# Output operands prepared as the merged tiles come, the merge's first pages loaded ahead of later weights, and four PSUM banks for the spatial mixing

## The chip, the cores and the metric

One core of one Trainium2 chip. The metric is the device time of one execution of the program in microseconds, the median of three runs.

## What is computed

One layer of a decoder block on a sequence of 1024 tokens of width 1024, all in float32. `h = rms_norm(x)` goes through one wide projection, which gives the inputs of three branches and three merge gates:

```python
u, v  -> y_a = (u * (causal spatial mixing of layer_norm(v) + bias)) * silu(a_z)   # 768 wide
q,k,v -> y_b = (dilated window attention, 3 patterns, combined) * silu(b_z)        # 256 wide
m_q   -> y_m = (attention into 256 memory tokens) * silu(m_z)                      # 512 wide
gates  = sigmoid(g.reshape(bn, s, 3, 1024) + gate_b)
merged = gates[0] * (y_a @ proj_a) + gates[1] * (y_b @ proj_b) + gates[2] * (y_m @ proj_m)
x      = x + merged @ w_out
```

## The kernel before

Every product of matrices in this part is made of three matmuls (`mm3`, L159 to L161): each operand is split into a high half (ACT, L137) and a low half (DVE, L138), and high x high, high x low and low x high are added in one PSUM bank. So each loaded weight piece (`piece`, load at L142 through SP's queue) and each page of `y` costs one operation of ACT and one of DVE before TensorE (PE) can use it. `pj` is the PSUM tag with four banks for the products; `sc` and `tr` are tags with two banks each. SP's DMA queue and each engine's queue run in order; that order is fixed when the program is built, mostly but not strictly by the order in the source.

From about 867 us to the end the kernel does the following.

The wide projection writes gate tiles and `y` pages to DRAM; its last pair of column tiles ends at 870 us. Then the merge runs in three passes over eight column tiles `dt` of the result, two halves `i` each, so 16 products a pass. `gates_m` (memory branch, 12 matmuls a product) loads the branch's first pages with `load_y(0, ...)` (L1109, tiles `ym00l` and `ym01l`, split by `split_y`), takes eight weight pieces pm0 to pm7 that were queued as `steps` (L1010) and multiplies by the gate tile `merged[dt]` in place (L1159). `gates(1, ...)` (window branch, 6 matmuls a product) and `gates(0, ...)` (gating branch, 18 matmuls) take a gate tile `tg` and weights from `prepare`, one tile ahead; DVE multiplies the product by the gate into `tg` (L1204), which also empties the PSUM bank; then the result is added to `merged[dt]`: by POOL in the second pass (L1208), and in the third pass by an accumulating DMA from POOL's queue (L1206) for tiles 0 to 6 and by DVE for tile 7 (L1208).

During the first two passes `spatial` makes the six `ya` tiles: matmuls into a `mx` bank (L1242), DVE scales and adds the bias (L1243, empties the bank), POOL multiplies by `us` (L1247), and `split` makes the halves `yah`/`yal` by ACT and DVE. `pump` releases these steps between the products of the passes.

The third pass runs over the tiles in the order 0, 4, 1, 5, 2, 6, 3, 7. After each one `merged_done` calls `right_sums`. The output projection is a seven-product scheme for blocks of 2 x 2: its right operands (1, 5, 3, 2, 6, 7, 4) are blocks of `merged` and sums of them, where tiles `k` and `k + 4` form a pair. `right_sums(k + 4)` makes for pair `k` the halves `ro1`, a subtraction (L1301), `ro5`, `ro3`, `ro2` and three more sums (L1305 to L1307); `half_split` makes the high half on ACT (L1288) and the low half on DVE (L1289). The operands 6, 7 and 4 follow with `right_late`, at once for pairs 0 and 1 and between the output's products for 2 and 3. `places` lists the buffer of each operand in the order of the calls: freed pages of the `y` tiles, freed merged tiles, and slices of `rpool`, whose two buffers held `ya0` and `ya1`. The left operands come from `w_out` by `next_steps`.

The output is a list of products (`jobs`), 12 matmuls of 256 columns each. The first four (rows 0 and 1, operands 1 and 5) run in two goes, `k` = 0 to 2 for all four and `k` = 3 after that (`partial`); they are written to the four `pj` banks that the last products of the third pass had. The results are added to the residual tiles `xr`, which take the three buffers of the `tg` ring, and stored.

## Time and profile before

| | |
|---|---|
| time, median of 3 runs | 1119.93 us (1119.44 to 1121.22) |
| the profiled execution | 1120.26 us, of it 1118.5 us span |
| mean granted clock of PE | 0.994 |
| busy share of the span | PE 98%, DVE 71%, ACT 46%, POOL 17% |
| DMA moved | 157.57 MB, 141 GB/s over the span |

The times of the rows below are from this one execution, counted from the start of its span. PE is the matmul engine, PEld its weight load, DVE the vector, ACT the scalar and POOL the GpSimd engine; SP's queue issues most of the loads. A row of the waits names the engine that stood still, its instruction, and behind the arrow the instruction whose end it waited for. A busy time is that of the instructions' own durations, and neighbours on one engine overlap a little.

### The profile page before, as it was taken

The page shows a single profiled execution, that of the slowest core. Times are in us where ns is not written, and L with a number is a line of the kernel's source. Part 1 is how long each engine was busy: PE and PEld are TensorE (multiplying, and loading weights), DVE is VectorE, ACT ScalarE, POOL GpSimd, SP SyncE. Part 2 cuts the span into 40 slices and gives each one's busy share as a digit, 9 for nine tenths or more (in the row PEclk, how much of TensorE's full clock was granted, in tenths as well). Part 3 has the DMA queues.
Part 4 walks back from the last instruction along what each step waited for, and adds up shares of the span by engine and source line. Part 5 has one row for each costly group of instructions (what it writes and reads, how often), then busy time and mean ns, then how long its engine had stood idle before and what let it go on. Part 6 is the DMA issues. An engine that isn't in the chain of part 4 may idle for free.

```text
span 1118.5 us, 18302 instructions
## 1 busy us (share of the span) xinstructions
PE 1092.7 (98%) x6680; PEld 955.9 (85%) x6680; DVE 794.1 (71%) x1701; ACT 514.0 (46%) x1123; POOL 195.7 (17%) x250
## 2 busy tenths in 40 slices
PE   8989999999999999999999999999999999998998
PEld 7879999999988887888888888888888787886998
DVE  6999899856687766656555656687885467568863
ACT  6553333223245543755665554666564562134320
POOL 0000431321000002011111111111111026511232
PEclk9999999999999999999999999999999999999999
DMA  7222322454242423444434325455544975665432
GB/s 236 76 96 91 128 86 96 144 190 151 72 142 94 129 98 119 143 147 153 128 121 136 124 95 181 123 180 157 166 132 132 335 273 160 173 161 136 142 107 83
DMA packets 84558, 157.57 MB, mean 141 GB/s; under 512 B 9605, under 2 KB 30708, under 8 KB 84468
## 3 DMA queue, kind: packets, MB, share of 16 engines
q1 hardware_dynamic: 68164, 106.87, 30.6%
q0 software_dynamic: 14864, 47.05, 13.0%
q10 hardware_dynamic: 1440, 2.49, 0.6%
q8 instruction: 52, 0.85, 0.3%
q14 instruction: 38, 0.31, 0.1%
HBM read 106.84 MB, written 48.22 MB: 139 GB/s over the span
## 4 chain that ended last, share of the span: by engine, by line
PE 86%; DVE 5%; DMA 4%; issue 3%; POOL 1%; ACT 1%; SPq 0%; POOLq 0%; DVEq 0%; ACTq 0%
PE t L159 12%; PE t L161 12%; PE t L160 11%; PE n L160 7%; PE n L159 7%; PE n L161 7%; PE po L606 3%; PE pp L159 2%; DMA merged<-tg 2%; PE pp L161 2%; PE pp L160 2%; PE po L160 2%; PE po L159 2%; PE po L161 2%; PE pt L599 1%
## 5 line engine op out<-in xcount | busy, mean ns | idle before, releaser
L159 PE MATMUL t<-th,wh_t 128*128 128x512 f32 x336 | 135.2, 402 | 0.0
L161 PE MATMUL t<-th,wl_t 128*128 128x512 f32 x336 | 132.0, 393 | 0.0
L160 PE MATMUL t<-tl,wh_t 128*128 128x512 f32 x336 | 131.4, 391 | 0.0
L159 PE MATMUL n<-wh_n,th 128*128 128x256 f32 x384 | 108.2, 282 | 0.0
L161 PE MATMUL n<-wh_n,tl 128*128 128x256 f32 x384 | 107.6, 280 | 0.0
L160 PE MATMUL n<-wl_n,th 128*128 128x256 f32 x384 | 107.6, 280 | 0.0
L161 PEld LDWEIGHTS t<-th,wl_t 128*128 128x128 f32 x336 | 63.1, 188 | 14.5
L159 PEld LDWEIGHTS n<-wh_n,th 128*128 128x128 f32 x384 | 73.3, 191 | 1.5 <-issue 0.9
L160 PEld LDWEIGHTS t<-tl,wh_t 128*128 128x128 f32 x336 | 63.3, 188 | 12.8
L159 PEld LDWEIGHTS t<-th,wh_t 128*128 128x128 f32 x336 | 63.3, 188 | 12.3
L160 PEld LDWEIGHTS n<-wl_n,th 128*128 128x128 f32 x384 | 72.1, 188 | 0.2 <-issue 0.2
L161 PEld LDWEIGHTS n<-wh_n,tl 128*128 128x128 f32 x384 | 72.2, 188 | 0.0
L159 PE MATMUL t<-H2h,wh_t 128*128 128x512 f32 x168 | 67.8, 404 | 0.0
L137 ACT CAST wh_t<-ws_t 128x512 fp32r<-128x512 f32 x86 | 51.8, 619 | 33.3 <-PE n L161 11.8
L161 PE MATMUL t<-H2h,wl_t 128*128 128x512 f32 x168 | 65.9, 392 | 0.0
L160 PE MATMUL t<-H2l,wh_t 128*128 128x512 f32 x168 | 65.5, 390 | 0.0
L138 DVE TENSOR_TENSOR wl_t<-ws_t,wh_t 128x512 fp32r<-128x512 f32 x86 | 58.2, 685 | 10.0 <-ACT wh_t L137 9.9
L1069 DVE TENSOR_TENSOR o<-t,sa 128x512 f32<-128x512 f32 x63 | 43.3, 687 | 29.5 <-PE t L161 25.1
L1038 POOL DMA_DIRECT2D scr_g<-o x48 | 26.1, 544 | 191.9 <-ACT o L1024 167.1
L939 POOL TENSOR_TENSOR on<-on,nss 128x1024 f32<-128x1024 f32 x12 | 26.2, 2205 | 173.4 <-DVE nss L134 116.0
L159 PE MATMUL n<-wh_n,H2h 128*128 128x256 f32 x192 | 54.9, 286 | 0.1
L160 PE MATMUL n<-wl_n,H2h 128*128 128x256 f32 x192 | 54.3, 283 | 0.0
(382 smaller groups left out, 3185.1 us busy)
## 6 DMA issues: line engine op xcount, KB each, us to landing
ws_t<-in_w_t SPq DMA_DIRECT2D x64, 256.0 KB, 3.5
scr_g<-o POOLq DMA_DIRECT2D x48, 256.0 KB, 2.7
tg<-scr_g SPq DMA_DIRECT2D x16, 512.0 KB, 3.9
ws_n<-in_w_n SPq DMA_DIRECT2D x24, 256.0 KB, 3.3
wr_n<-in_w_n SPq DMA_DIRECT2D x24, 256.0 KB, 3.3
scr_qk<-on POOLq DMA_DIRECT2D x12, 512.0 KB, 4.3
bx<-scr_qk SPq DMA_DIRECT2D x24, 256.0 KB, 3.3
wr_t<-in_w_t SPq DMA_DIRECT2D x20, 256.0 KB, 3.5
```

The lines of the kernel that those rows point to most:

```text
L137: A.copy(out=hi, in_=y)
L138: (eng or V).tensor_tensor(out=lo, in0=y, in1=hi.bitcast(F32), op=ALU.subtract)
L159: T.matmul(o, lhsT=ah, rhs=bh, start=first, stop=False)
L160: T.matmul(o, lhsT=ah, rhs=bl, start=False, stop=False)
L161: T.matmul(o, lhsT=al, rhs=bh, start=False, stop=last)
L599: T.transpose(p2[:, h * P:(h + 1) * P], c.pr[h // 2][:, h % 2, b * P:(b + 1) * P], ident)
L606: T.matmul(po[:, 64 * h:64 * h + 64], lhsT=c.pT[b][:, h * P:(h + 1) * P], rhs=mb.v[:, (t - nk + 1 + b) % 3, 64 * h:64 * h + 64], start=b = ...
L939: G.tensor_tensor(out=v, in0=v, in1=ss[:, 16 * ORD[q]:16 * ORD[q] + 16].unsqueeze(2) .to_broadcast([P, 16, 64]), op=ALU.mult)
L1038: G.dma_start(out=t[:, h], in_=d)
L1069: V.tensor_tensor(out=o[q], in0=psum, in1=s, op=ALU.add)
```

## The change

The program has the same matmuls in the merge and in the output. (A) Only pm0 to pm3 are queued as steps; pm4 to pm7 and the first `prepare` of each later pass are issued after the DMA of `ym01l` (`issue_after`). (B) The `mx` products alternate between the tags `sc` and `tr`. (C) `right_sums` makes operands 1 and 5 of pair `k` when tile `k` is merged and the rest when tile `k + 4` is, each handed out one tile behind except after tiles 3 and 7; tile 3 is added by DVE as tile 7 was; operands 1 and 5 of pair 3 lie in the `tg` ring; the first four output products run `k` = 0 to 3 in one go; the residual tiles take two slices of one `rpool` buffer; and the sum `s` of the left operands is split from the two that follow it, so that piece 5 of the output comes before them.

```diff
--- before.py
+++ after.py
@@ -336,9 +336,11 @@
             for b in blocks:
                 w[b] = load((11, 21, 22, 12).index(b))
 
-        def sums():
+        def first():
             w["s"] = extra()
             V.tensor_tensor(out=w["s"], in0=w[21], in1=w[22], op=ALU.add)
+
+        def rest():
             V.tensor_tensor(out=w[21], in0=w[11], in1=w[21], op=ALU.subtract)
             V.tensor_tensor(out=w[11], in0=w["s"], in1=w[11], op=ALU.subtract)
 
@@ -346,7 +348,7 @@
             V.tensor_tensor(out=w[12], in0=w[12], in1=w[11], op=ALU.subtract)
 
         return {"load": lambda: loads(11, 12, 21, 22), "11": lambda: loads(11), "12": lambda: loads(12),
-                "2": lambda: loads(21, 22), "sums": sums, "last": last,
+                "2": lambda: loads(21, 22), "s": first, "rest": rest, "last": last,
                 1: lambda: ready(w[11], 1), 2: lambda: ready(w[12], 2), 3: lambda: ready(w[12], 3), 4: lambda: ready(w[22], 4), 5: lambda: ready(w["s"], 5),
                 6: lambda: ready(w[11], 6), 7: lambda: ready(w[21], 7)}
 
@@ -402,7 +404,7 @@
         n = len(ps_)
         ahead.append(ps_)
         nxt = len(ahead)
-        steps.extend((n, step(*keys)) for keys in ((1,), (2,), ("sums", 6), (7, ("11",)), (5,), (4, ("12",)),
+        steps.extend((n, step(*keys)) for keys in ((1,), (2,), ("s", "rest", 6), (7, ("11",)), (5,), (4, ("12",)),
                                                    ("last", 3, ("2",))))
 
     tstack = ExitStack()
@@ -1007,7 +1009,7 @@
         V.scalar_tensor_tensor(out=avs[:, KT:], in0=mv[:, :, 0], scalar=-1.0, in1=avs[:, :KT],
                                op0=ALU.mult, op1=ALU.mult)
 
-    for dt in range(KT):
+    for dt in range(4):
         steps.append((1, lambda dt=dt: prepared.append(piece(w_pm[dt], 512, f"p2{dt}"))))
 
     with tc.tile_pool(name="ppool", reuse_waits="tile", bufs=1, side="right") as pp_:
@@ -1106,7 +1108,7 @@
 
         places.append([[page([P, 2, 512], f"{name}{i}{hp}{d}", F32R) for hp in range(n)] for d in "hl"])
         for hp in range(n):
-            nc.sync.dma_start(out=places[i][1][hp].bitcast(F32), in_=scr[:, 2 * hp:2 * hp + 2, 512 * i:512 * i + 512])
+            last[0] = nc.sync.dma_start(out=places[i][1][hp].bitcast(F32), in_=scr[:, 2 * hp:2 * hp + 2, 512 * i:512 * i + 512])
 
     def split_y(i, places, k):
         hi, lo = (places[i][d][k // 2][:, k % 2, :] for d in range(2))
@@ -1130,6 +1132,7 @@
         nc.sync.dma_start(out=merged[dt][:, t], in_=scr_g[2][dt][:, t])
 
     load_y(0, ym, scr_ym, 2, "ym")
+    first_pages = last[0].ins
     for i in range(4):
         split_y(0, ym, i)
     for dt in range(KT):
@@ -1143,12 +1146,16 @@
 
     def gates_m():
 
-        w = []
+        w, late_w = [], deque()
         for i in range(2):
             t = slice(512 * i, 512 * i + 512)
             for dt in range(KT):
-                if i == 0:
+                if i == 0 and dt < 4:
                     w += take(1, 4)
+                    with tc.issue_after(first_pages):
+                        late_w.append(piece(w_pm[dt + 4], 512, f"p2{dt + 4}"))
+                elif i == 0:
+                    w.append(late_w.popleft())
                 pp = ps.tile([P, 512], F32, name=f"pp2{dt}{i}", tag="pj", bufs=4)
                 for k in range(4):
                     c = slice(k * P, (k + 1) * P)
@@ -1188,7 +1195,8 @@
                 wk_ += [(ph[:, c * P:(c + 1) * P], pl[:, c * P:(c + 1) * P]) for c in range(n)]
             ahead.append((tg, wk_))
 
-        prepare(order[0])
+        with tc.issue_after(first_pages):
+            prepare(order[0])
         for n, dt in enumerate(order):
             if n + 1 < KT:
                 prepare(order[n + 1])
@@ -1202,7 +1210,7 @@
                     pump()
                 m = merged[dt][:, t]
                 V.scalar_tensor_tensor(out=tg[:, t], in0=tg[:, t], scalar=1.0, in1=pp, op0=ALU.add, op1=ALU.mult)
-                if br == 0 and dt < 7:
+                if br == 0 and dt not in (3, 7):
                     G.dma_start(out=m, in_=tg[:, t], accum_op=ALU.add)
                 else:
                     (G if br else V).tensor_tensor(out=m, in0=m, in1=tg[:, t], op=ALU.add)
@@ -1233,7 +1241,7 @@
                                      for d in "hl"))
                 yas.append(lambda half, y=yav[i]: tuple(a[:, 512 * half:512 * half + 512] for a in y))
             yh, yl = yav[i]
-            pm = ps.tile([P, 512], F32, name=f"mx{i}{h}", tag="sc")
+            pm = ps.tile([P, 512], F32, name=f"mx{i}{h}", tag=("sc", "tr")[h])
             mt = p1([P, 512], f"mt{i}{h}", "mt", 2)
             for c4 in range(4):
                 j = 4 * h + c4
@@ -1265,6 +1273,7 @@
     tq = ctx.enter_context(tc.tile_pool(name="tq", reuse_waits="tile", bufs=1))
     pg = lambda pool: lambda n: pool.tile([P, 2, 512], F32R, name=n, tag="pg")
     mg = lambda n: p1([P, 2, 512], n, "mg", 8, tm, F32R)
+    tg_place = lambda n: p1([P, 2, 512], n, "tg", 3, tm, F32R)
     rp = []
 
     def half_r(n):
@@ -1275,8 +1284,8 @@
         return rp[-1][:, 1]
 
     places = ([pg(ypool)] * 8 + [pg(t2)] * 2 + [lambda n: p1([P, 2, 512], n, "pg", 3, tq, F32R)] * 3 + [pg(t2)]
-              + [mg] * 4 + [half_r] * 4 + [pg(ypool)] * 5 + [pg(t2)])
-    spare = [pg(t2)] * 2 + [mg] * 2 + [lambda n: p1([P, 2, 512], n, "tg", 3, tm, F32R)]
+              + [mg] * 4 + [tg_place] * 2 + [half_r] * 2 + [pg(ypool)] * 5 + [pg(t2)])
+    spare = [pg(t2)] * 2 + [mg] * 2 + [tg_place]
     right_o = {}
     late = deque()
     PORDER = (1, 5, 3, 2, 6, 7, 4)
@@ -1292,14 +1301,15 @@
 
     def right_sums(dt):
 
+
+        k = dt % 4
+        b11, b12 = merged[k][:, 0:512], merged[k][:, 512:S]
         if dt < 4:
+            right_o[1, k] = half_split(b11, f"ro1{k}")
+            V.tensor_tensor(out=b11, in0=b12, in1=b11, op=ALU.subtract)
+            right_o[5, k] = half_split(b11, f"ro5{k}")
             return
-        k = dt - 4
-        b11, b12 = merged[k][:, 0:512], merged[k][:, 512:S]
         b21, b22 = merged[dt][:, 0:512], merged[dt][:, 512:S]
-        right_o[1, k] = half_split(b11, f"ro1{k}")
-        V.tensor_tensor(out=b11, in0=b12, in1=b11, op=ALU.subtract)
-        right_o[5, k] = half_split(b11, f"ro5{k}")
         right_o[3, k] = half_split(b22, f"ro3{k}")
         right_o[2, k] = half_split(b21, f"ro2{k}")
         V.tensor_tensor(out=b12, in0=b22, in1=b12, op=ALU.subtract)
@@ -1337,7 +1347,7 @@
     def next_steps(c, n):
 
         for p in osteps[c]:
-            for key in ((1,), ("sums", 5), (2, "last", 3), (), (6,), (7,), (4,))[n]:
+            for key in ((1,), ("s", 5), ("rest", 2, "last", 3), (), (6,), (7,), (4,))[n]:
                 p[key]()
 
     def begin(c):
@@ -1346,8 +1356,13 @@
             p["load"]()
         next_steps(c, 0)
 
+    waiting = []
+
     def merged_done(dt):
-        right_sums(dt)
+
+        waiting.append(dt)
+        while waiting and (dt in (3, 7) or len(waiting) > 1):
+            right_sums(waiting.pop(0))
         if dt == 3:
             begin(0)
             next_steps(0, 1)
@@ -1357,34 +1372,19 @@
     late = deque(sorted(late, key=lambda t: PORDER.index(t[0])))
     jobs = [(0, j, n) for js in ((0, 1), (2, 3)) for ns in (range(2), range(2, 7)) for j in js for n in ns]
     jobs += [(1, j, n) for j in range(4) for n in range(7)]
+    xrs = rpool.tile([P, 2, 2, 512], F32, name="xrs", tag="r")
     tiles = {}
     done = 3
-
-    def partial(c, j, n, ks):
-        q = PORDER[n]
-        if (c, j, n) not in accs:
-            accs[c, j, n] = ps.tile([P, 512], F32, name=f"po{c}{j}{q}",
-                                    **(dict(tag="sc") if q in (2, 3) else dict(tag="pj", bufs=4)))[:, :256]
-        acc = accs[c, j, n]
-        for k in ks:
-            r, (lh, ll) = right_o[q, k], left_o[q, k // 2]
-            w = slice(256 * (k % 2), 256 * (k % 2) + 256)
-            t = slice(j * P, (j + 1) * P)
-            mm3(acc, r[:, 0, t], r[:, 1, t], lh[:, w], ll[:, w], k == 0, k == 3)
-        return acc
-
-    accs = {}
-    for job in jobs[:4]:
-        partial(*job, range(3))
     for c, j, n in jobs:
         if n == 0:
-            xr = p1([P, 2, 512], f"xr{c}{j}", "tg", 3, tm)
+            xr = xrs[:, j % 2]
             for h in range(2):
                 nc.sync.dma_start(out=xr[:, h, :], in_=x[512 * h + j * P:512 * h + (j + 1) * P, 512 * c:512 * c + 512])
             tiles[c, j] = xr, p1([P, 4, 256], f"sm{c}{j}", "mg", 8, tm)
         xr, sm = tiles[c, j]
         sa, sd = sm[:, 0, :], sm[:, 1, :]
         o11, o21, o12, o22 = xr[:, 0, 0:256], xr[:, 0, 256:512], xr[:, 1, 0:256], xr[:, 1, 256:512]
+        t = slice(j * P, (j + 1) * P)
         q = PORDER[n]
         if (c, j) == (0, 0):
             while done < min(n + 3, 6):
@@ -1392,7 +1392,11 @@
                 next_steps(0, done)
         while late and n > 1 and late[0][0] == q:
             right_late(1)
-        acc = partial(c, j, n, range(3 if (c, j, n) in accs else 0, 4))
+        acc = ps.tile([P, 512], F32, name=f"po{c}{j}{q}", **(dict(tag="sc") if q in (2, 3) else dict(tag="pj", bufs=4)))[:, :256]
+        for k in range(4):
+            r, (lh, ll) = right_o[q, k], left_o[q, k // 2]
+            w = slice(256 * (k % 2), 256 * (k % 2) + 256)
+            mm3(acc, r[:, 0, t], r[:, 1, t], lh[:, w], ll[:, w], k == 0, k == 3)
         if (c, j) == (0, 3):
             if n == 0:
                 begin(1)
```

## Rows read from the trace of the kernel before

**Rows 1.** the page's first part: busy time of an engine, share, instructions
```profile
PE 1092.7 (98%) x6680; PEld 955.9 (85%) x6680; DVE 794.1 (71%) x1701; ACT 514.0 (46%) x1123; POOL 195.7 (17%) x250
```

**Rows 2.** waits of PE, 860 us on: releaser, us in total, times, longest
```profile
PE po L159 <- DVE tg L1204: 5.2, 2, 2.9
PE pp L159 <- ACT ym00h L137: 2.3, 1, 2.3
PE mx L1242 <- DVE mt L1243: 2.2, 1, 2.2
...
PE pp L159 <- DVE tg L1204: 0.3, 1, 0.3
```

**Rows 3.** window: length, busy PE PEld DVE ACT POOL; clock, DMA share, GB/s
```profile
872.40:876.70 4.30, 4.30 (x12) 3.38 (x13) 2.56 (x4) 2.12 (x4) 0.54 (x1) 0.61 1.03 384
```

**Rows 4.** windows: the third merge, and from its end into the output
```profile
967.00:1021.90 54.90, 54.62 (x239) 44.46 (x238) 33.19 (x55) 14.57 (x27) 10.17 (x13) 1.00 0.67 159
1021.90:1047.00 25.10, 18.34 (x116) 17.23 (x116) 23.57 (x40) 12.47 (x23) 5.21 (x7) 0.86 0.45 125
```

**Rows 5.** timeline of SP's queue: start, duration, what is issued, number
```profile
860.40 6.42 SPq L142 DMA_DIRECT2D ws_p<-in_w_pb  x3
866.87 0.43 SPq L1109 DMA_DIRECT2D ym00l<-scr_ym  x1
867.35 0.46 SPq L1109 DMA_DIRECT2D ym01l<-scr_ym  x1
867.85 3.11 SPq L1130 DMA_DIRECT2D merged<-scr_g  x3
```

**Rows 6.** the tile ym00l: ns min/median/max of its split; its landing
```profile
L137 ACT CAST ym00h<-ym00l x2: 604/611/618, 871.7 to 872.9; 128x512 fp32r<-128x512 f32 x2
L138 DVE TENSOR_TENSOR ym00l<-ym00l,ym00h x2: 693/693/693, 872.4 to 873.5; 128x512 fp32r<-128x512 f32 x2
...
DMA to landing us min/median/max: 4.8/4.8/4.8
```

**Rows 7.** timeline of PE in the projection's last pair
```profile
858.43 0.39 PE L160 MATMUL t<-tl,wh_t 128*128 128x512 f32 x1
858.66 0.39 PE L161 MATMUL t<-th,wl_t 128*128 128x512 f32 x1
```

**Rows 8.** waits of the other engines, 860 us to the end
```profile
POOL mt L1247 <- DMA us<-scr_us: 28.3, 1, 28.3
...
DVE yal L138 <- ACT yah L137: 11.5, 8, 3.1
...
DVE merged L1305 <- DMA merged<-tg: 7.5, 3, 4.6
```

**Rows 9.** timeline of DVE in the second merge
```profile
948.60 0.68 DVE L1204 SCALAR_TENSOR_TENSOR tg<-tg,pp 128x512 f32<-128x512 f32 x1
...
950.19 0.67 DVE L1204 SCALAR_TENSOR_TENSOR tg<-tg,pp 128x512 f32<-128x512 f32 x1
...
953.69 0.67 DVE L1204 SCALAR_TENSOR_TENSOR tg<-tg,pp 128x512 f32<-128x512 f32 x1
...
956.20 0.67 DVE L1204 SCALAR_TENSOR_TENSOR tg<-tg,pp 128x512 f32<-128x512 f32 x1
```

**Rows 10.** timeline of PE in the second merge and at the third's start
```profile
950.33 1.16 PE L1242 MATMUL mx<-spw,VV 128*128 128x128 f32 x8 [2.21 <-DVE mt L1243]
...
957.03 0.46 PE L159 MATMUL pp<-ya,wh_p 128*128 128x512 f32 x1
```

**Rows 11.** timeline of DVE where the output begins
```profile
1026.26 0.68 DVE L1204 SCALAR_TENSOR_TENSOR tg<-tg,pp 128x512 f32<-128x512 f32 x1
...
1028.90 0.69 DVE L1208 TENSOR_TENSOR merged<-merged,tg 128x512 f32<-128x512 f32 x1
...
1033.03 0.68 DVE L1204 SCALAR_TENSOR_TENSOR tg<-tg,pp 128x512 f32<-128x512 f32 x1
```

**Rows 12.** the accumulating DMAs of L1206, issue to landing
```profile
DMA to landing us min/median/max: 3.2/3.6/9.7
```

## The prediction

> **What bounds the kernel now.** I read four views in this order. The page's first part says that TensorE (PE) is busy in 98% of the span [rows 1], so a change that adds no matmul and removes none can only gain where PE stands still, or where it runs slowly behind a standstill. The view of PE's waits from 860 us on tells where that is [rows 2]: 2.3 us for the high half of the merge's first page (`ym00h`), 2.2 us for a PSUM bank of the spatial mixing (`mx`), 5.2 us in two goes for banks that DVE has not yet emptied (`po`), and 0.3 us of the same kind one stage earlier (`pp`); two smaller ones in the output I leave out. The windows then show a second price: in the 4.3 us behind the first stall the granted clock is 0.61 of full [rows 3], that is, partly the lower of the two levels (1.2 GHz of 2.4), after PE had stood for 2.3 us. The columns that went through would have taken 0.61 x 4.3 = 2.6 us, so the stall cost 4.3 - 2.6 = 1.7 us more. From 1021.9 to 1047 the clock is 0.86 over 25.1 us [rows 4]: 3.5 us, about two such drops, behind the two `po` stalls. I take 1.7 us for each of four drops. All stalls and drops together are 2.3 + 2.2 + 5.2 + 0.3 + 1.7 + 1.7 + 3.5 = 16.9 us: about the most that the change can bring. Last I read the queues of SP and DVE around each stall, to see what stands behind it.
>
> **First pages ahead of later weights (stall at 870.1 us).** SP's queue is one line: the three loads of `w_pb` occupy it from 860.40 for 6.42 us, since each waits for its slot, then `ym00l` goes at 866.87, `ym01l` at 867.35 and the gate tiles from 867.85 [rows 5]. `ym00l` lands 4.8 us after its issue, ACT makes its high half in 0.61 us, DVE its low half in 0.69 [rows 6]. It overwrites a page that the last pair of the projection reads: by the program its release is the matmul at 858.43 [rows 7], so without the loads ahead of it it could go some 8 us earlier. `ym01l` waits for a product that ends just before its issue, and can't move. The change defers pm4 to pm7 and the first `prepare` of the second merge behind `ym01l`'s issue. Then `ym00l` is there long before 870.1, when PE runs dry (it resumes at 872.4, where the window of [rows 3] begins, less the 2.3 of [rows 2]). `ym01` is needed after 12 matmuls of 0.23 us [rows 7], at 872.8; it lands at about 867.35 + 4.8 = 872.15, its high half at 872.8, its low half at 873.5, one matmul later than needed: 0 to 0.7 us of waiting, I take 0.3. Sum: -2.3 - 1.7 + 0.3 = -3.7 us.
>
> What moved behind costs nothing if it is in time. pm4 is due after four products of 12 matmuls, 870.1 + 48 x 0.23 = 881.1. Its slot is free, so it should be issued at about 867.5, with the gate tiles. The moved loads are five of 0.26 MB; at the 384 GB/s of this stretch [rows 3] they take 3.4 us, so even the last is split by 877, and the covers are the products of pm0 to pm3, 11 us. What lands behind is 3.4 us later: gate tiles, the second pages, and the first `us` tile, for which POOL waited 28.3 us [rows 8]. POOL has slack there for several us. If it hadn't, all 3.7 would go. Bounds for this part: -4.0 to 0 (if pm4 queues behind all gate tiles, see the rivals, +3).
>
> **Four banks for the spatial mixing (stall at 948.1).** It adds nothing: the two banks called "tr" lie idle there. The stalled matmuls write the last mixing tile; they start at 950.33 after 2.2 us and take 1.2 us [rows 10]. With four banks they would start at 948.1. The question is what is late next. The gate products rotate through four banks of their own, and DVE empties them at 948.60, 950.19, 953.69 and 956.20, each in 0.68 us [rows 9]. The next four products need those banks in this order. With no stall PE would run the mixing to about 949.2 and one gate product (six matmuls of 0.23 us, 1.4 us) from 949.3. The next would run from 950.9 to 952.3, the third from 954.4, when its bank is empty, to 955.8, and the next stage would begin at 956.9, with the fourth bank. It begins now at 957.03 [rows 10]. So 0.1 us is gained: what holds DVE back is its wait for ACT's high halves of the mixing (11.5 us in eight times, [rows 8]), which in turn wait for POOL's multiply, and these don't hang on the bank. The stall only moves to 952.3. I take 0; the bounds are -3.9 (2.2 and a drop of 1.7) and +0.5, for one more short stall in a place where the clock is full now.
> The Trainium skill, in "Perfetto Trace Analysis", section "Matmul Optimizations", advises to have all eight PSUM banks in use so that more instructions can run side by side. By that rule the whole stall would go; the eviction times of [rows 9] speak against it.
>
> **The output's operands (stalls at 1024.8 and 1030.9).** The total of DVE's work is nearly the same. Added are two adds for tile 3, of 0.69 us each [rows 11], for two accumulating DMAs of POOL's queue, which landed 3.2 to 9.7 us after issue, 3.6 in the median [rows 12]. Moved: for tile pairs 0 to 2 the first operand, the subtraction and the fifth come where they were, one tile behind the merge; the third, second and three sums come one tile later than now, so that DVE's wait for the accumulates at L1305 (7.5 us in three times, [rows 8]) may shrink. For pair 3 they come ahead of tile 7's merge, and into the ring of gate tiles, not into `rpool`, whose buffers the last product still reads. The first four output products no longer run three quarters first: each does its 12 matmuls at once and so needs the operands of tile 3.
>
> Where is the limit? From 1021.9 to 1047 DVE is busy 23.57 of 25.10 us, PE 18.34 [rows 4]. PE waits because DVE empties the last gate banks as late as 1026.26 and 1033.03 [rows 11]; these evictions stand in one line with the operands' halves and left operands. From 967 to 1021.9 DVE is busy only 33.19 of 54.90 us [rows 4], but it idles behind accumulates in its own order: eviction, accumulate, subtraction, eviction. I expect the order of that queue in pairs 0 to 2 to stay much as it is, since the program's position of the waiting subtraction, L1301, relative to the merge doesn't change. Then the backlog at 1021.9 remains, and the change at the end is small: +1.4 for the adds; -1.5 for DVE's idle time there (25.10 - 23.57), which is waiting for accumulates and for PE's partial products; -1.7 for one of the two clock drops, since whole products run on once they start and one stall takes the place of two. Sum -1.8 us. The residual tiles now take two slices of one buffer instead of three: a load of tile j + 2 waits for the store of j, some 7 products of 1.4 us = 10 us earlier, which covers a load and a store; 0. Bounds: +2.8 (the adds' 1.4, and the first product waiting 1.4 longer for tile 3's halves) to -10.3, which is all of PE's idle time (25.10 - 18.34 = 6.8) and the drops (3.5), if DVE's 21.7 idle us before 1021.9 absorb the backlog.
>
> **Sum.** The profiled execution took 1120.26 us (span 1118.5), 0.33 above the median of the runs. 1120.26 - 3.7 - 0 - 1.8 = 1114.8; on the median, 1114.4.
>
> **The rivals.**
> *More goes than I say.* With each subtraction and half one tile behind, DVE never waits for an accumulate, is level with PE at 1023, and banks are free when the output begins. For it: 40% of DVE is idle in that stage. Against it: queue order. Time: 1114.4 + 1.8 - (6 to 10) = 1106 to 1110; with the mixing's 3.9 too, 1103 at best. About 1108.
> *The four banks pay.* The round trip of the second merge speeds up when a mixing tile can be computed before the last one is emptied, so that evictions come earlier too. For it: the stall is PE's own, and the round trip begins with the mixing. Against it: the eviction times of [rows 9] leave 0.1 us. Time: 1114.4 - 3.9 = 1110.5. The Trainium skill's rule on the eight banks, cited above, would have this one.
> *Only one part pays.* First pages in time and the end as it is: 1116.2 on the median. Or the reverse, 1118.
> *Neither pays.* PE's gain at 870 is met by a stage whose pace is set by POOL's `us` tile and the round trip POOL, ACT, DVE, and the end is DVE's. Then 1119 to 1121, no change. For it: the evictions, not PE, set the time from 948 on. Against it: the `us` load and the products that feed the chain come earlier with PE.
> *Slower.* Place: the third merge, 957 to 1023. Evictions lag there until PE's four banks are just used up, with one stall of 0.3 us in that pass (`pp`, [rows 2]). If the new order puts the early operands (two halves and a subtraction, about 1.8 us) in front of an eviction in each of the last three pairs, all of it reaches PE from that point on: 3 x 1.8 = 5.4, behind two stalls a drop each, 3.4, so +8.8, less the 3.7 at 870: 1125 us. It decides from the first 0.3 us of added lag. Against it: the total of operations per pair is the same, and they are handed out later, not earlier. Smaller in the same direction: pm4 queued behind eight gate tiles and the second pages (5.2 MB, 14 us at 384 GB/s, so split at about 883 to 886 against 881.1) costs 2 to 5 us and a drop, which uses up the gain at 870 and up to 3 more.
>
> **How the numbers follow.** Forecast (1112 to 1116 us): 0.40. More goes: 0.16. The four banks pay: 0.07. One part pays: 0.16. Neither: 0.11. Slower: 0.10. The range leaves out the slower rival and the lowest tip of the first: 1104 to 1121. 0.2%, or 2.2 us, is about what a measurement of this kernel tells from no change (its runs span 0.16%). Faster than 1117.7: 0.40 + 0.16 + 0.07 + most of the one-part cases, 0.14 = 0.77; within: 0.12; slower: 0.11.
>
> **What would show it.** First pages: no wait on `ym00h`, the `ym00l` load before 860, clock 1.0 at 873; wrong, if PE waits for `wh_p` near 881. Mixing: no `mx` wait, but a `pp` wait on DVE's `tg` near 952 and the next stage beginning at the same distance from 870 as now. End: DVE still over 90% busy for 20 us behind the last gate product, one `po` stall and one drop. The prediction is wrong if evictions follow their products within 3 us at 1015 to 1023 (then it is the first rival), or if `pp` waits appear there (the last).

## The result, and the profile after

The changed kernel takes 1125.64 us in the median (1124.43 to 1130.62, 7 runs) against 1119.53 us (7 runs) before: ratio 1.0059, interval 1.0039 to 1.0078. It is slower by about 6 us where the forecast was 5.5 us faster.

Where that is, is read best by passes. Each column is a difference of two times in PE's timeline: the projection's last matmul, the first matmul on a `yb` page (the second pass begins), the first on a `ya` page (the third begins), the end of the third pass, and the last matmul. The stall ahead of pass 1 is part of pass 1. The times are those of one profiled execution of each kernel, the ratios those of all its runs. All times in the text with a plus sign count from the projection's last matmul or from the end of the third pass, as named.

| kernel | stall ahead of pass 1 | pass 1 | pass 2 | 1 + 2 | pass 3 | output | ratio to before, interval |
|---|---|---|---|---|---|---|---|
| before | 2.3 | 53.2 | 33.8 | 87.0 | 66.7 | 90.4 | |
| changed | none | 54.3 | 35.6 | 89.9 | 67.7 | 93.2 | 1.0059, 1.0039 to 1.0078 |
| e1: first part only | none | 54.6 | 35.0 | 89.5 | 67.4 | 90.5 | 1.0032, 1.0020 to 1.0044 |
| e2: banks only | 1.9 | 51.3 | 34.1 | 85.4 | 67.0 | 90.3 | 1.0010, 0.9996 to 1.0024 |
| e3: output part only | 2.5 | 51.8 | 34.4 | 86.3 | 66.9 | 92.8 | 1.0035, 1.0022 to 1.0048 |
| e4: only the prepare late | none | 50.1 | 36.2 | 86.3 | 66.6 | 90.5 | 1.0000, 0.9986 to 1.0014 |
| e5: third pass's adds on DVE | 2.4 | 51.8 | 33.8 | 85.5 | 66.1 | 81.5 | 0.9906, 0.9885 to 0.9926 |
| e6: e4, half of pass 2's adds on DVE | none | 50.1 | 34.9 | 84.9 | 66.5 | 90.4 | 0.9993, 0.9981 to 1.0006 |
| e7: e5 and e6 | none | 50.1 | 35.1 | 85.2 | 66.1 | 81.6 | 0.9891, 0.9869 to 0.9912 |
| e8: e3, tile 3 by DMA | 1.8 | 51.2 | 34.1 | 85.3 | 67.1 | 96.6 | 1.0056, 1.0036 to 1.0076 |
| e9: changed, third pass's adds on DVE | none | 54.2 | 34.4 | 88.7 | 66.2 | 81.4 | 0.9939, 0.9917 to 0.9961 |
| e10: e3, first products in parts | 1.8 | 52.7 | 33.8 | 86.5 | 68.4 | 92.0 | 1.0020, 1.0005 to 1.0035 |
| e11: before, tile 3 on DVE | 2.0 | 51.3 | 33.9 | 85.3 | 66.6 | 91.2 | 0.9995, 0.9981 to 1.0009 |
| e12: e7 and the banks | none | 50.1 | 34.8 | 84.8 | 66.1 | 81.6 | 0.9901, 0.9881 to 0.9921 |
| e13: e4, first `us` tile early | none | 50.1 | 34.5 | 84.5 | 66.4 | 90.5 | 0.9978, 0.9965 to 0.9991 |
| e14: e7, first `us` tile early | none | 50.1 | 32.7 | 82.8 | 66.1 | 81.6 | 0.9860, 0.9843 to 0.9876 |
| e15: e7 without the late prepare | 1.8 | 51.1 | 33.7 | 84.8 | 66.1 | 81.5 | 0.9890, 0.9874 to 0.9906 |

From before to after the passes add 1.1 + 1.9 + 1.0 + 2.8 us, 6.7 before rounding. The profiled execution of the changed kernel, 1129.17 us, is longer by 2.1 us more, and these lie ahead of the projection's last matmul, whose end varies more than that (868.9 to 873.6 us) between the profiles of the other kernels here.

How far single profiles can be trusted shows where kernels share code. The six that leave the output as it was (before, e1, e2, e4, e6, e13) take 90.3 to 90.5 us there. The seven others that leave pass 1 as it was (e2, e3, e5, e8, e10, e11, e15) take 51.1 to 52.7 us in it, against 53.2 in the profile of before: that one has a drop of the clock in pass 1 that six of the seven don't have. So its columns "pass 1" and "1 + 2" are some 1.5 to 2 us higher than those of most executions, and the change's loss in the first two passes is rather about 4 us than 2.9.

The five largest waits of PE in the changed kernel (columns as in [rows 2]):

```profile
PE pp L159 <- DVE tg L1212: 4.9, 6, 1.8
PE mx L1250 <- ACT VV L1224: 2.2, 1, 2.2
PE po L159 <- DVE tg L1212: 1.7, 2, 0.9
PE po L159 <- ACT ro L1297: 1.7, 1, 1.7
PE po L159 <- ACT wo L137: 1.1, 2, 0.9
```

Against [rows 2]: the wait for `ym00h` is gone, and so is the one for the mixing's bank (`mx` behind `mt`). In their places stand six waits of the gate products for banks (`pp`, 4.9 us in place of 0.3) and one wait of a mixing product for its `VV` tile. Four of the six lie inside the second pass and one, of 1.0 us, at its end; in the third pass there is one of 0.3 us, as before. The output's waits for banks shrank from 5.2 to 1.7 us, but there is a new one for an operand (`ro`). SP's queue at the head of the first pass, as [rows 5]:

```profile
860.98 0.38 SPq L1111 DMA_DIRECT2D ym00l<-scr_ym  x1
869.22 0.38 SPq L1111 DMA_DIRECT2D ym01l<-scr_ym  x1
869.65 6.43 SPq L1132 DMA_DIRECT2D merged<-scr_g  x8
876.18 0.81 SPq L142 DMA_DIRECT2D ws_p<-in_w_pm  x1
...
881.06 2.07 SPq L142 DMA_DIRECT2D ws_p<-in_w_pm  x1
...
883.70 0.38 SPq L142 DMA_DIRECT2D ws_p<-in_w_pm  x1
...
885.14 0.33 SPq L142 DMA_DIRECT2D ws_p<-in_w_pm  x1
```

`ym00l` goes 8.2 us ahead of `ym01l`, as forecast. The four held-back weights do not go next: all eight gate tiles stand ahead of the first of them, and second pages and `VV` tiles ahead of the others.

The windows behind the third pass, 25.1 us from 1.8 us ahead of its end, as the second row of [rows 4] (e5's begins 1.4 ahead). In the changed kernel:

```profile
1028.00:1053.10 25.10, 19.49 (x106) 17.04 (x105) 23.94 (x42) 11.84 (x23) 3.41 (x5) 0.80 0.32 104
```

The same window of e3, the output part alone:

```profile
1021.90:1047.00 25.10, 19.20 (x106) 17.04 (x105) 23.95 (x42) 11.84 (x23) 3.40 (x5) 0.78 0.32 104
```

The same window of e5, the best single edit:

```profile
1021.30:1046.40 25.10, 23.79 (x191) 22.94 (x191) 22.88 (x44) 8.69 (x17) 6.21 (x8) 1.00 0.36 111
```

Before, 116 matmuls went through here at a clock of 0.86; the changed kernel and e3 get 106 through at 0.80 and 0.78; e5 gets 191 through at 1.00. DVE is busy for 23 to 24 us in all four. So DVE's busy time doesn't tell the good case from the bad ones; what its operations wait for does, as e5 shows below.

### The profile page after: what moved, and what is told of

Same layout as the page of the kernel before. It is cut to its first block, busy times and chain, and to the rows that moved or that the text cites. A ratio compares the mean times of both kernels' runs of the same rounds, so it can differ in the third digit from the quotient of the medians.

```text
span 1127.4 us, 18275 instructions
## 1 busy us (share of the span) xinstructions
PE 1100.5 (98%) x6680; PEld 960.2 (85%) x6680; DVE 797.6 (71%) x1703; ACT 514.5 (46%) x1123; POOL 195.5 (17%) x248
## 4 chain that ended last, share of the span: by engine, by line
PE 83%; DMA 6%; DVE 5%; issue 3%; POOL 1%; ACT 1%; SPq 0%; DVEq 0%; POOLq 0%; ACTq 0%
PE t L159 11%; PE t L161 11%; PE t L160 11%; PE n L160 7%; PE n L159 7%; PE n L161 7%; PE po L608 3%; PE po L159 2%; PE po L161 2%; PE po L160 2%; DMA merged<-tg 1%; PE pt L601 1%; PE pp L159 1%; PE po_m L752 1%; PE pp L160 1%
## 5 line engine op out<-in xcount | busy, mean ns | idle before, releaser
L137 ACT CAST wh_t<-ws_t 128x512 fp32r<-128x512 f32 x86 | 51.8, 619 | 33.3 <-PE t L160 11.9
L1026 ACT ACTIVATE o<-o,gb 128x512 f32<-128x512 f32 x48 | 34.7, 724 | 49.5 <-DVE o L1071 47.9
```

The costliest lines, as they stand in the source:

```text
L137: A.copy(out=hi, in_=y)
L1026: A.activation(out=d, in_=d, func=AF.Tanh, scale=0.5, bias=gb[:, col:col + 1])
```

## The experiments

**Each part alone.** Three kernels that have one part of the change each; e1 is the held-back weights and the first prepare, e2 the tag of the mixing, e3 all the rest.

> Only the first part of the change: four weight pieces and the first prepare of the later passes behind the first pages. In the changed kernel the standstill at the head of the first pass went, but four weight pieces came behind eight gate tiles and the first mixing product stood 2.2 us for its VV tile. Theory 1 (each part pays or costs in its own pass): the first pass (from the projection's last matmul to the second pass's first) takes 54.3 us as in the changed kernel against 53.2 before, the later ones as before: 1121 us. Theory 2 (the late loads push everything behind them: weight splits fall into the second pass, evictions lag, the output starts late): second pass 35 to 36 us against 33.8, output also longer: 1124 to 1126 us.

> Only the four banks of the spatial mixing. Both theories as in the prediction: the stall on the mixing's bank moves to the gate products' banks, second pass 33.4 to 34.0 us against 33.8, total within 1 us of before. Theory 1 has it slower if the second pass is 35.6 us as in the changed kernel: 1122 us.

> Only the output's operands. Theory 1: third pass 67.5 us against 66.5 and the output from its first product to its last 93.4 against 90.6, as in the changed kernel: 1123.5 us. Theory 2: without the late loads the third pass and the output go as forecast, 1117 to 1119 us.

e1 costs 1.0032, most of it in passes 1 and 2 (89.5 us against 87.0), with 0.7 us in the third pass, and its output is as before (90.5). So the first part is a loss by itself, and neither of its theories holds whole: the loss is not pass 1's alone (theory 1 had the later passes as before and 1121 us), and the output is not longer (theory 2 had it so). e2 is the same as before: the mixing's wait is gone, and four bank waits of 2.7 us in all stand in its place, where there was one of 0.3. e3 costs 1.0035: third pass nearly unchanged (theory 1 had 67.5 us), output 2.4 us longer. So two parts lose, each by itself, and the output's loss is the third part's alone. What the three parts cost one by one, 0.0032, 0.0010 and 0.0035, adds up to 0.0077, and the whole change costs 0.0059, with 0.0078 as the upper end of its interval.

**What in the first part costs.** e4 defers only the prepare; pm0 to pm7 stay queued as steps, all eight early. Against the kernel before, in excerpts (the line that sets `last[0]` is the one in the change):

```diff
     load_y(0, ym, scr_ym, 2, "ym")
+    first_pages = last[0].ins
...
-        prepare(order[0])
+        with tc.issue_after(first_pages):
+            prepare(order[0])
```

> Of the first part only the deferred first prepare; all eight weight pieces of the first pass are loaded early as before. The load of the first page was held up by the three loads of that prepare and of nothing else (they occupied SP's queue from 860.4 to 866.9). Theory 1: the standstill of 2.3 us and its clock drop go, no mixing product is sent ahead, so the first pass takes 49.5 us against 53.2 and the rest stays: 1116.5 us. Theory 2: the weight splits of the second pass still fall later, so 2 us of it are given back there: 1118 to 1120 us.

The stall is gone in e4 as in e1, pass 1 takes 50.1 us in place of 54.6. What differs in PE's waits there is one, in e1 of 2.3 us; here in the timeline of PE in the changed kernel:

```profile
889.19 1.61 PE L1250 MATMUL mx<-spw,VV 128*128 128x128 f32 x6 [2.21 <-ACT VV L1224]
890.47 0.79 PE L159 MATMUL pp<-ym00h,wh_p 128*128 128x512 f32 x1
891.06 0.63 PE L160 MATMUL pp<-ym00l,wh_p 128*128 128x512 f32 x1
```

and the window behind it, as [rows 3]:

```profile
889.19:893.50 4.31, 4.31 (x15) 3.75 (x16) 2.04 (x3) 4.24 (x10) 0.00 (x0) 0.60 1.11 345
```

Before, the first mixing product runs at 899.52, +29.5 us behind the projection; here it stands in PE's queue at +17.0, inside the first half of pass 1, and waits for a `VV` tile. The tile isn't late: ACT's first operation on one begins at +16.5 in both kernels (886.52 and 888.65). It is the product that is early. Matmuls behind it take up to 0.79 us in place of 0.39, and the granted clock is 0.60 for 4.3 us, that is 1.7 us more; with the wait, 3.9 of the 4.2 us by which the pass is longer than in e4. It stands there in the three kernels with the four weights held back (e1, e9, the changed one: 2.2 to 2.4 us each) and in none of the others. No product waited for the weights themselves. That the order of PE's queue changed is seen; that it did because the weights' loads come later in the program's order is inferred from these three against the rest.

**But e4 is no faster than before.** It gains the stall in pass 1, 1.0 to 1.7 us against the six kernels that have the stall and no drop behind it, and gives it back in pass 2 (36.2 us against 33.8), where gate products wait 2.1 us for banks. That is less than either of its theories had. Two things were tried for what paces the second pass: e6 takes half of its adds off POOL, e13 loads POOL's first `us` tile right behind the first pages. Both keep the edit of e4. In excerpts (in e13 the mixing's own load step also takes this tile in place of loading it):

```diff
-                    (G if br else V).tensor_tensor(out=m, in0=m, in1=tg[:, t], op=ALU.add)
+                    (G if br and i else V).tensor_tensor(out=m, in0=m, in1=tg[:, t], op=ALU.add)   # e6
...
     first_pages = last[0].ins
+    us0 = p1([P, S], "us0", "us", 3)                                                               # e13
+    nc.sync.dma_start(out=us0, in_=scr_us[0])
```

> The deferred prepare of the run before, and the second pass's adds of half 0 on DVE instead of POOL (8 adds of 0.69 us). Theory: the second pass is paced by the round trip DVE eviction, POOL add, POOL multiply, ACT half, DVE half (0.68 + 1.29 + 1.5 + 0.62 + 1.1 = 5.2 us a tile), not by PE, so that standstills taken from PE ahead of it come back as waits; without one POOL add in the trip the second pass takes 31 to 34 us against 36.2, and the third pass begins at 81 to 84 us behind the projection against 86.3. Rival: DVE's or the transfers' own time bounds it: 86 us as it was.

> The deferred prepare, and the first us tile loaded right behind the first pages. The tile landed 31 us after the projection's end, and POOL stood 28 us for it. If its landing anchors the passes, the third pass begins 2 to 4 us earlier than with the deferred prepare alone (86.3 us after the projection): 82 to 84, total 1117 to 1119 us. If the round trip of the second pass and DVE's queue set the pace, POOL's wait goes to the next mixing tile (DVE delivers its second one at 35 us) and the third pass begins at 85.5 to 87: 1120 to 1121 us.

e6 takes the third pass's start from +86.3 to +84.9, less than expected: DVE's wait for ACT's halves falls from 8.4 (e4) to 3.8 us in the second pass, but PE still stands 2.4 us for the mixing's bank and 2.2 for gate banks; POOL is busy 17.1 us of the pass in place of 25.9, and DVE 30.6 of 34.8. e13 brings +84.5, between the ranges of its two theories, and a ratio of 0.9978, below 1 by its interval. POOL's timeline tells (multiplies of the mixing, in brackets the idle time ahead and what ended it). The first one before:

```profile
902.14 1.29 POOL L1247 TENSOR_TENSOR mt<-us,mt 128x512 f32<-128x512 f32 x1 [28.34 <-DMA us<-scr_us]
```

The first one in the changed kernel:

```profile
906.23 1.30 POOL L1255 TENSOR_TENSOR mt<-us,mt 128x512 f32<-128x512 f32 x1 [31.67 <-DMA us<-scr_us]
```

The first two in e4:

```profile
902.84 1.28 POOL L1249 TENSOR_TENSOR mt<-us,mt 128x512 f32<-128x512 f32 x1 [29.51 <-DMA us<-scr_us]
906.83 1.29 POOL L1249 TENSOR_TENSOR mt<-us,mt 128x512 f32<-128x512 f32 x1 [2.71 <-DVE mt L1245]
```

The first two in e13:

```profile
898.88 1.29 POOL L1254 TENSOR_TENSOR mt<-us,mt 128x512 f32<-128x512 f32 x1 [25.86 <-DMA merged<-scr_g]
905.28 1.28 POOL L1254 TENSOR_TENSOR mt<-us,mt 128x512 f32<-128x512 f32 x1 [5.11 <-DVE mt L1250]
```

From the projection's end (870.06, 872.19, 870.96 and 870.65 in the four) that is +32.1, +34.0, +31.9 and +28.2; the second multiply of e4 and e13 comes at +35.9 and +34.6. So without an earlier load the tile's landing sets when the first multiply can begin, and a stall taken away ahead of it doesn't move it (before and e4: +32.1 and +31.9). It isn't the whole: in e13, whose load is issued at 873.06, the first multiply no longer waits for the tile but follows DVE's scaling of the mixing tile, which ends at 898.79; it comes 3.7 us earlier than in e4, the second multiply 1.2, the third pass 1.7.

**What holds up the output.** e5 is the kernel before with one change: every add of the third pass is done by DVE.

```diff
-                if br == 0 and dt < 7:
-                    G.dma_start(out=m, in_=tg[:, t], accum_op=ALU.add)
-                else:
-                    (G if br else V).tensor_tensor(out=m, in0=m, in1=tg[:, t], op=ALU.add)
+                (G if br else V).tensor_tensor(out=m, in0=m, in1=tg[:, t], op=ALU.add)
```

> The kernel before, with all adds of the third pass on DVE instead of POOL's accumulating DMAs (14 adds of 0.69 us more for DVE, 14 DMAs less). Theory 2 now: what the output waits for is not the total of DVE's work but the accumulates' landing inside DVE's queue (7.5 us at the sums, 5.4 at the subtraction before). Then evictions keep up with the products, the first output products find their banks, and from the third pass's end to PE's last matmul it takes 83 to 87 us against 90.4: 1113 to 1117 us. Theory 1, that DVE's total work bounds the end: 9.7 us more of it, 91 to 95 us, 1122 to 1126.

0.9906, 10.8 us less in the medians, and more than expected: 8.9 us of it in the output, 0.6 in pass 3 and 1.1 behind the last matmul. DVE has 14 operations more, and PE's waits for banks at the head of the output are gone altogether. Its waits from 860 us on:

```profile
PE pp L159 <- ACT ym00h L137: 2.4, 1, 2.4
PE mx L1239 <- DVE mt L1240: 2.2, 1, 2.2
PE po L159 <- ACT wo L137: 1.1, 1, 1.1
PE po L159 <- DVE xr L1400: 0.2, 1, 0.2
```

and DVE's own waits from 967 to 1024 us, in its third pass (before, the sums alone waited 7.5 us there for accumulates, [rows 8], the subtraction at L1301 another 5.0):

```profile
DVE ro L1286 <- ACT ro L1285: 2.1, 3, 0.7
DVE tg L1204 <- PE pp L161: 1.7, 3, 0.9
DVE so L341 <- DMA ws_o<-in_w_o: 0.2, 1, 0.2
```

DVE now waits for PE's products, which is how a queue that keeps up looks. The last eviction shows it best (DVE's timeline; before it began at 1033.03, [rows 11], 9.3 us behind the pass's end at 1023.73). The sum ahead of it, before:

```profile
1021.91 0.69 DVE L1305 TENSOR_TENSOR merged<-merged,merged 128x512 f32<-128x512 f32 x1 [2.52 <-DMA merged<-tg]
```

DVE's timeline of e3, whose pass ends at 1023.74:

```profile
1021.35 0.69 DVE L1309 TENSOR_TENSOR merged<-merged,merged 128x512 f32<-128x512 f32 x1 [2.52 <-DMA merged<-tg]
...
1034.41 0.68 DVE L1206 SCALAR_TENSOR_TENSOR tg<-tg,pp 128x512 f32<-128x512 f32 x1
```

The last two evictions of e5, whose pass ends at 1022.66:

```profile
1018.57 0.69 DVE L1204 SCALAR_TENSOR_TENSOR tg<-tg,pp 128x512 f32<-128x512 f32 x1 [0.90 <-PE pp L161]
...
1023.06 0.68 DVE L1204 SCALAR_TENSOR_TENSOR tg<-tg,pp 128x512 f32<-128x512 f32 x1
```

In e3 the sum still waits 2.52 us for an accumulate in the midst of the queue, exactly as long as in the kernel before, and the last eviction comes at +10.7 in place of +9.3: 1.4 us later, as much as the two adds take. In e5 it comes at +0.4. Whether adds on POOL, as in the second pass, would do as well as adds on DVE was not run.

**Inside the output part.** Of e3, e8 takes back the adds of tile 3 and e10 the whole first products; e11 puts the adds of tile 3 alone into the kernel before. In excerpts, with the base of each named:

```diff
-                if br == 0 and dt not in (3, 7):    # e3
+                if br == 0 and dt < 7:              # e8
+    for job in jobs[:4]:
+        partial(*job, range(3))                     # e10, with partial as before
-                if br == 0 and dt < 7:              # before
+                if br == 0 and dt not in (3, 7):    # e11
```

> The output part of the change alone, but tile 3 is added by the accumulating DMAs as before. In the output part alone the last gate bank was emptied 1.4 us later than before, just the two adds, and PE's stall behind the left operand (1.8 us against 1.1) had a clock drop of 3.6 us behind it. Theory 1 (the adds): without them the output takes 90.5 to 91.5 us as before instead of 92.8. Rival (the whole products at the head): they wait for tile 3's operands anyway, and longer, since these now wait for the accumulate: 92.5 to 95 us.

> The output part alone, but its first four products run three quarters first, as before. Theory A (whole products at the head cost, since the second waits for tile 3's halves while the others' work would be ready): output 89 to 91 us against 92.8. Theory B (the two adds and the reordering cost): 92.5 to 93.5.

> The kernel before, with tile 3 alone added by DVE: one line of the change. As forecast: two adds of 0.69 us put the last eviction 1.2 to 1.4 us later, the output takes 91.5 us against 90.4. By theory 2 a gain of the accumulate's latency, and of the wait for tile 3's subtraction, is possible: 88 to 90.

e8 has the longest output of all, 96.6 us; of its waits, one line tells why:

```profile
PE po L159 <- ACT ro L1291: 7.8, 2, 5.6
```

The whole products wait for tile 3's halves, and those for the accumulate. So the adds on DVE, which I had as a cost, save 3.7 us of the output inside the changed order, and the whole products are what made them necessary. In the kernel before, where the first three quarters cover for tile 3, the same adds are worth nothing (e11, 0.9995, with the output 0.8 us longer). e10 lies between e3 and before (1.0020), its output 0.8 us shorter than e3's and its third pass 1.5 longer; by its interval it can't be told from e3, so how the loss of the output part splits between whole products and the earlier place of the operands stays open.

e9 asks what is left of the output part once the accumulates are gone:

```diff
-                if br == 0 and dt not in (3, 7):
-                    G.dma_start(out=m, in_=tg[:, t], accum_op=ALU.add)
-                else:
-                    (G if br else V).tensor_tensor(out=m, in0=m, in1=tg[:, t], op=ALU.add)
+                (G if br else V).tensor_tensor(out=m, in0=m, in1=tg[:, t], op=ALU.add)
```

> The changed kernel with all adds of the third pass on DVE. Theory 2 (the accumulates inside DVE's queue are the cause at the end): the waits at the head of the output go, from the third pass's end to the last matmul it takes 81 to 83 us as in the kernel before with these adds, against 93.2; the first two passes stay 3 us longer than before. 1112 to 1115 us. Rival (the order in which the change hands out the operands costs by itself): 85 to 90 us in the output, 1116 to 1121.

Nothing: pass 3 and output take 66.2 and 81.4 us with the change's order of operands, 66.1 and 81.5 without it (e5). What remains of the change is the loss in passes 1 and 2.

**Together.**

> Both together with the deferred prepare: half of the second pass's adds and all of the third's on DVE. If both theories hold, the gains add up: third pass begins 2 to 5 us earlier and the output takes 83 to 87 us: 1109 to 1115 us. If one bound is DVE's work, less than the better of the two alone.

> The fastest version so far (deferred prepare, half of the second pass's adds and all of the third's on DVE), and the four banks for the spatial mixing. With the shorter round trip the mixing's bank (1.5 us) and the gate products' banks (2.2 us) both stop PE in the second pass. If banks now decide, the second pass takes 32 to 34 us against 35.1: 1107 to 1109 us. If DVE's evictions still do, the stall moves again: 35 us, 1109.6.

> Half of the second pass's adds and all of the third's on DVE, without the deferred prepare: the standstill of 2.3 us at the head of the first pass is back. If the second pass swallows what PE gains ahead of it, the third pass begins at 85 us as with the deferral, 1109.6 us; if the deferral pays once the second pass is relieved, 86.5 to 87.5, 1111.5 us.

> The same early tile in the version with half of the second pass's adds and all of the third's on DVE and the deferred prepare. Anchor: third pass begins at 82 to 84 us instead of 85.2, 1107 to 1108 us. Round trip and DVE: 84.5 to 85.5, 1109.5 us.

e7 is 0.9891 and hardly better than e5; the four banks add nothing to it (e12: the mixing's wait of 1.5 us is gone, gate banks 4.2 us in place of 2.2), and the deferred prepare neither (e15 is at +84.8 without it, e7 at +85.2). With the `us` tile early as well, e14 begins the third pass at +82.8 and takes 1106.32 us, ratio 0.9860 (0.9843 to 0.9876). This is the fastest version here, ahead of both kernels.

## Why the prediction was wrong

*First pages.* The step "the stall goes" was right, and so was the load 8 us earlier. Three steps behind it failed. "What moved behind costs nothing if it is in time": the weights were in time, their first high half made 10.8 us behind the projection's end with 11 us allowed, by luck rather than by the 4 us that I had reckoned, since they did not go "with the gate tiles" but behind them. But holding them back went with another order of PE's queue, which the sum didn't have: a mixing product 12.5 us earlier, ahead of its `VV` tile, 2.2 us and a drop of 1.7. "POOL has slack there for several us": it has none, since the first `us` tile's landing decides when its first multiply begins (+34.0 in place of +32.1). I had named the case ("if it hadn't, all 3.7 would go") and given it too little. And the 3.7 us themselves counted a clock drop of 1.7 that does not always follow (below). So the -3.7 became about +3.6 (e1, 1.0032).

*Four banks.* Right, the term of 0 and its mechanism: in e2 the `mx` wait turns into `pp` waits on DVE's evictions, 2.7 us in place of 2.2, and the kernel is the same by its interval. The place to which I moved the stall I had taken to be at full clock; before, the clock is 0.67 there, in the 4.3 us behind the mixing's stall. The Trainium skill ("Perfetto Trace Analysis", "Matmul Optimizations") asks for all eight banks to be in use; read as a rule by which the stall and its drop go, it would have had 3.9 us here. The run decides against that in this place, and again in e12.

*Output.* The step "the order of that queue stays much as it is" held in the wait that matters: e3's sum waits the same 2.52 us as before. The adds' 1.4 us fits: the last bank comes 1.4 us later (in e11, which has the adds alone, the output is 0.8 us longer). What failed is the two terms that made the sum negative. Of "-1.5 for DVE's idle time" only 0.4 came: DVE is busy 23.95 us of that window in place of 23.57, and the two adds alone are 1.4. "-1.7 for one of the two clock drops, since one stall takes the place of two" was the reverse: whole products wait for an operand and for two banks in turn, the stalls are shorter but more. PE stands still for 0.9 us less in that window (19.20 us busy in place of 18.34), but the clock is 0.78 in place of 0.86, 25.1 x 0.08 = 2.0 us more lost. So -1.8 became +2.4, near the upper bound of +2.8 that I had given this part.

*The rival that came true* is none of those named whole. Its parts were: "neither pays" for the passes 1 and 2 as far as `us` is concerned, and the upper bound of the output. The slower rival that I priced, evictions stopping PE in the third pass, did not come: PE's wait for banks inside that pass is 0.3 us, as before, and the pass is 1.0 us longer (67.7 against 66.7) in place of 8.8, with 0.7 us of waiting behind ACT's halves of output operands in it. That its 1125 us is nearly the measured time is luck. The upper bounds of the parts, 3 + 0.5 + 2.8, added up to 1126.6; the range ended at 1121, because I gave each part's loss a chance of its own and never the case that two parts lose together.

*What I passed over.* The rows had it: DVE idle for 21.7 us of the third pass while it is the bound behind it, 7.5 us of it behind accumulates in three waits; another 5.0 at the subtraction, in the same profile, make 12.5. I took that order as given and sized the change against it. The question should have been which operation puts a transfer's latency (3.6 us in the median, [rows 12]) into the middle of DVE's line; doing it on DVE costs 14 x 0.69 = 9.7 us of work in a stage where 21.7 are idle, and gives 10.8 us.

## What to carry to other kernels

An engine that is 94% busy behind a stage and 60% busy inside it, as DVE is here, can be short of order and not of work time: look in its queue for the operation that waits for a transfer, and price doing that work on the engine itself against the transfer's latency. A standstill taken away ahead of a stage is worth only what the latest other input of that stage allows, so look up when each input lands (here POOL's `us` tile) before counting the gain. And where the program's order is fixed when it is built, and not strictly by the source, an edit that holds back a load can come with products moved on another engine, as in e1; the price of that must be looked for in the wait lists afterwards, since the diff doesn't show it.

## What the runs showed of the hardware

A stall of about 2 us is not always followed by a drop of the clock. The head of the first pass stood for 1.8 to 2.5 us in eight of the profiles above; behind it the clock fell in two (before, 2.3 us; e10, 1.8) and not in six, among them the longest. The window behind it in e5, which had stood for 2.4 us, to be held against [rows 3]:

```profile
873.49:877.80 4.31, 4.31 (x19) 3.54 (x20) 2.65 (x5) 2.12 (x4) 0.54 (x1) 1.00 1.05 381
```

19 matmuls at 1.00 in the time in which before ran 12 at 0.61. PE had run without a gap ahead of the stall in both. At the wait for the mixing's bank in the second pass it is the other way round: 13 kernels here have it, with 1.5 to 2.4 us, and in the 4.3 us behind it the clock was 0.60 to 0.67 in ten of them and 1.00 in e6, e7 and e14. Behind the wait for the early `VV` tile it fell in all three. What makes the difference is open. So the 1.7 us is a price with a chance, which is another one at each place, not a part of the stall; here it made up 1.7 of the 3.7 us that I counted at the first pages and nearly all of the 1.8 at the output, and a single profile of before can't tell it.
